# Early weight slabs loaded one step ahead of their split, with their steps spread over both products of a feed-forward half

## The chip, the cores and the metric

The kernel runs on one core of a Trainium2 chip. Its engines are TensorE (PE: matmuls, and PEld: their weight loads), VectorE (DVE), ScalarE (ACT), GpSimd (POOL) and SyncE (SP), each with its own instruction queue, and 16 DMA engines that move data between HBM and the core's memory. The metric is the time of one execution on the device in microseconds, the median of several runs.

## The reference

A decoder trunk of two layers over 256 tokens of width 1024, all in float32. Each layer is a half-step feed-forward block, a mixer of three attention branches, and a second half-step feed-forward block:

```python
def swiglu_ffn(x, g, wi, wo):
    a, b = jnp.split(rms_norm(x, g) @ wi, 2, axis=-1)
    return (jax.nn.silu(a) * b) @ wo

for l in range(DEPTH):
    x = x + 0.5 * swiglu_ffn(x, ffn1_norm[l], ffn1_wi[l], ffn1_wo[l])
    h = rms_norm(x, mix_norm[l])
    ...  # stick-breaking, latent and sparse attention on h @ w_in, gated sum y
    x = x + y @ w_out[l]
    x = x + 0.5 * swiglu_ffn(x, ffn2_norm[l], ffn2_wi[l], ffn2_wo[l])
```

The inner width DFF is 2816, so wi is 1024 x 5632 and wo is 2816 x 1024.

## The kernel before

Precision. Every float32 operand of a matmul is split into a high part, rounded to TensorE's fast float32 type by a copy on ScalarE, and a low part, the rest, by a subtraction on VectorE. A product is then three matmuls (high by high, high by low, low by high) that add up in one PSUM bank. So all weights go through ScalarE and VectorE too, not only through TensorE.

Weights. They stream in a fixed order as slabs of 128 partitions x up to 1024 columns. A slab is loaded in two raw halves of 512 columns (`load_raw`, six buffers named raw) from SyncE's queue, and each half is split into the slab's tiles: whi/wlo from the pool wp, four buffers that live through the whole kernel, or vhi/vlo from the pool fp, four buffers that live for one feed-forward half. `slab_tiles` decides: the slabs 4 to 43 of a half use vhi/vlo, the first four and the 22 slabs of wo use whi/wlo. `next_slab` keeps two slabs loaded beyond the one it gives out. A raw half's buffer is free again when its subtraction on VectorE is done, and a slab's tiles are free when TensorE has used the slab.

A feed-forward half (`ffn`, run four times: two per layer). In words, it has three parts.

- Eight steps: the first 256 columns of both parts of wi (slabs 0 to 3), for each of the two row tiles t of 128 tokens: 24 matmuls of 512 columns each. Behind the last step of a tile, `glu` makes the SiLU on ScalarE (tile sil) and the gate product g on VectorE.
- The first product: five chunks of 512 columns of wi, first the gate part and then the value part of each, so ten drains of four slabs. It runs transposed (`chunk_T`): the weights are stationary, the 256 tokens are the moving operand, and each drain yields eight times (i = 0 to 7) after 12 matmuls of 256 columns. Between two yields a hook may put other work in. For the first drain it puts in `flush` at i = 3 and i = 5 (four transposes in all, that bring g into the transposed layout, split into gh and gl) and `spread_rn` at i = 4: the row scales of the norm are broadcast to a tile rnb on VectorE and transposed, for each row tile in turn; rnb has one buffer, so the second copy waits for the first transpose and the second transpose for the second copy. The result `rows` is what `gate_T` multiplies by at the end of each gate drain.
- The second product (`out_rows`): 22 slabs of wo, 12 matmuls of 512 columns each, with gh and gl stationary.

Early slabs. The mixer's weights are heavy on ScalarE and VectorE, so for ten of its slabs per list in `EARLY_AT` the split is done ahead, in a feed-forward half before it (`split_early`): load a half to eraw, copy to ehi on ScalarE, subtract to elo on VectorE, and store both to HBM from GpSimd's queue. The mixer later loads them straight to whi/wlo. One early half is one step of the generator `ahead`; there are 20 steps in each of the first three feed-forward halves, none in the last. The load is held in SyncE's queue behind the last raw load emitted before it (`issue_after(last_dma[0])`). Before, `hook2` makes a step at i = 2 and i = 6 of every drain (in the very first half not in the first chunk), and `between` makes the four that are left in the first half's second product.

Order. TensorE's order is the program's (`manual_schedule`). In the feed-forward halves a list scheduler with its own estimate of times sets the order on VectorE, ScalarE, GpSimd and SyncE; in the mixer, `Planner` does for VectorE and ScalarE too. The scheduler may move an instruction forward past others of the program.

## Time and profile before

| | |
|---|---|
| median of 3 runs | 1289.9 us (1288.9 to 1293.35) |
| the profiled execution, its time | 1291.65 us |
| its span | 1289.9 us |
| TensorE busy | 1269.0 us (98%) |
| VectorE, ScalarE, GpSimd busy | 917.5, 787.8, 107.4 us |
| matmuls | 8103 records |
| read from HBM, written to it | 257.22 MB, 34.60 MB |

The span runs from the first to the last instruction; the execution's own time has 1.75 us more around it. Busy time of TensorE is counted from the start of a matmul to its modelled end, and neighbours overlap, so a busy TensorE can still start its matmuls at different distances. A row of the time line has the start in us from the span's start, the length, the engine, the line of the kernel, the tiles as out<-in, and in brackets the idle time before it with what ended it. A row of waits has the waiting instruction, what it waited for, the total in us, how often, and the longest.

### The profile page before, as it was taken

How to read it: one execution, taken by the hardware profiler on the slowest of the kernel's cores; microseconds unless marked ns; L12 is line 12 of the kernel's file. 1: busy time of each engine (PE TensorE's matmuls, PEld its weight loads, DVE VectorE, ACT ScalarE, POOL GpSimd, SP SyncE). 2: the span in 40 equal slices, each digit the busy share in tenths (PEclk: the TensorE clock that was granted, in tenths of full speed). 3: DMA queues.
4: the chain of work that ended last, by engine and by line, in shares of the span. 5: the costliest groups of instructions: out<-in, count | busy, mean ns of one | idle time of the engine just before them, and what ended most of it. 6: DMA issues, size and time to landing. Idle time of an engine off the chain costs nothing. (4 is left out here: it accounts for less than half of the span.)

```text
span 1289.9 us, 23603 instructions
## 1 busy us (share of the span) xinstructions
PE 1269.0 (98%) x8103; PEld 1127.0 (87%) x8103; DVE 917.5 (71%) x1934; ACT 787.8 (61%) x1644; POOL 107.4 (8%) x170
## 2 busy tenths in 40 slices
PE   7999999999999999999999999999999999999998
PEld 6999888888877889998889998888888778899987
DVE  6667667888898776776568765679768887666643
ACT  6555557777877565655456664578757774544542
POOL 0112100210000011220012210011100000000000
PEclk9999999999999999999999999999999999999999
DMA  7899876656645568997579996575786455566653
GB/s 234 286 318 324 292 265 219 196 168 218 205 126 170 168 230 299 338 328 247 177 263 345 326 323 198 187 228 157 246 289 223 141 168 166 180 183 193 214 164 115
DMA packets 151401, 293.93 MB, mean 228 GB/s; under 512 B 17768, under 2 KB 19440, under 8 KB 151280
## 3 DMA queue, kind: packets, MB, share of 16 engines
q1 hardware_dynamic: 141424, 260.43, 62.8%
q0 software_dynamic: 9856, 31.99, 6.6%
q8 instruction: 63, 1.03, 0.3%
q14 instruction: 58, 0.48, 0.1%
HBM read 257.22 MB, written 34.60 MB: 226 GB/s over the span
## 5 line engine op out<-in xcount | busy, mean ns | idle before, releaser
L758 PE MATMUL acc<-hThi,vhi 128*128 128x256 f32 x1280 | 356.7, 279 | 0.0
L760 PE MATMUL acc<-hThi,vlo 128*128 128x256 f32 x1280 | 356.5, 279 | 0.0
L759 PE MATMUL acc<-hTlo,vhi 128*128 128x256 f32 x1280 | 355.9, 278 | 0.0
L539 DVE TENSOR_TENSOR vlo<-raw,vhi 128x512 fp32r<-128x512 f32 x320 | 207.5, 686 | 62.5 <-ACT vhi L538 59.9
L538 ACT ACTIVATE vhi<-raw 128x512 fp32r<-128x512 f32 x320 | 188.4, 623 | 91.7 <-PE acc L759 35.5
L759 PEld LDWEIGHTS acc<-hTlo,vhi 128*128 128x128 f32 x1280 | 240.5, 188 | 0.1
L758 PEld LDWEIGHTS acc<-hThi,vhi 128*128 128x128 f32 x1280 | 240.3, 188 | 0.2
L760 PEld LDWEIGHTS acc<-hThi,vlo 128*128 128x128 f32 x1280 | 240.1, 188 | 0.3 <-DVE vlo L539 0.2
L539 DVE TENSOR_TENSOR wlo<-raw,whi 128x512 fp32r<-128x512 f32 x240 | 155.1, 686 | 110.4 <-ACT whi L538 110.0
L538 ACT ACTIVATE whi<-raw 128x512 fp32r<-128x512 f32 x240 | 138.7, 622 | 125.2 <-PE acc L586 94.7
L584 PE MATMUL acc<-whi,hThi 128*128 128x512 f32 (+2 forms) x480 | 189.9, 396 | 0.0
L586 PE MATMUL acc<-whi,hTlo 128*128 128x512 f32 (+2 forms) x480 | 184.6, 385 | 0.1
L585 PE MATMUL acc<-wlo,hThi 128*128 128x512 f32 (+2 forms) x480 | 183.9, 383 | 0.2 <-DVE wlo L539 0.2
L979 DVE TENSOR_TENSOR wlo<-raw,whi 128x512 fp32r<-128x512 f32 x216 | 141.0, 679 | 25.6 <-ACT whi L977 24.5
L977 ACT ACTIVATE whi<-raw 128x512 fp32r<-128x512 f32 x216 | 126.3, 617 | 39.0 <-PE acc L586 22.5
L584 PE MATMUL acc<-whi,gh 128*128 128x512 f32 x352 | 137.6, 391 | 0.0
L586 PE MATMUL acc<-whi,gl 128*128 128x512 f32 x352 | 137.0, 389 | 0.0
L585 PE MATMUL acc<-wlo,gh 128*128 128x512 f32 x352 | 137.0, 389 | 0.0
L586 PEld LDWEIGHTS acc<-whi,hTlo 128*128 128x128 f32 x480 | 90.6, 189 | 18.9 <-DVE ss L590 0.9
L584 PEld LDWEIGHTS acc<-whi,hThi 128*128 128x128 f32 x480 | 91.0, 190 | 15.7 <-issue 1.1
L585 PEld LDWEIGHTS acc<-wlo,hThi 128*128 128x128 f32 x480 | 91.1, 190 | 14.5 <-DVE wlo L539 0.6
L565 ACT ACTIVATE ehi<-eraw 128x512 fp32r<-128x512 f32 x60 | 37.8, 630 | 103.1 <-DMA eraw<-in_wts 102.8
(305 smaller groups left out, 1872.3 us busy)
## 6 DMA issues: line engine op xcount, KB each, us to landing
raw<-in_wts SPq DMA_DIRECT2D x764, 256.0 KB, 3.1
eraw<-in_wts SPq DMA_DIRECT2D x60, 256.0 KB, 5.3
early<-ehi POOLq DMA_DIRECT2D x60, 256.0 KB, 4.2
early<-elo POOLq DMA_DIRECT2D x60, 256.0 KB, 4.8
whi<-early SPq DMA_DIRECT2D x60, 256.0 KB, 4.0
wlo<-early SPq DMA_DIRECT2D x60, 256.0 KB, 3.9
gain<-in_gains SPq DMA_DIRECT2D x5, 512.0 KB, 5.7
xd<-x SPq DMA_DIRECT2D x4, 512.0 KB, 4.3
```

The source lines that it names most:

```text
L538: nc.scalar.activation(hi[:, c:c + m], raw[:, :m], AF.Copy)
L539: nc.vector.tensor_tensor(lo[:, c:c + m], raw[:, :m], hi[:, c:c + m], op=OP.subtract)
L565: nc.scalar.activation(hi, raw, AF.Copy)
L584: nc.tensor.matmul(o, a[0], b[0], start=start, stop=False)
L585: nc.tensor.matmul(o, a[0], b[1], start=False, stop=False)
L586: nc.tensor.matmul(o, a[1], b[0], start=False, stop=stop)
L758: nc.tensor.matmul(o, sl[0][:, w], h, start=k == 0 and c == 0, stop=False)
L759: nc.tensor.matmul(o, sl[0][:, w], l_, start=False, stop=False)
L760: nc.tensor.matmul(o, sl[1][:, w], h, start=False, stop=k == KT - 1 and c == 1)
L977: nc.scalar.activation(hl[0][:, c:c + m], raw[:, :m], AF.Copy)
L979: nc.vector.tensor_tensor(hl[1][:, c:c + m], raw[:, :m], hl[0][:, c:c + m], op=OP.subtract)
```

## The change

Five edits, all for the feed-forward halves.

1. `split_early` is one step deeper: a step loads its half and then finishes (copy, subtraction, stores) the half that the step before loaded. One more step at the end finishes the last, so there are 21.
2. The steps are placed anew: one per drain (i = 6) in the first three chunks, two per drain (i = 2 and 6) in the last two, and one at every odd slab k < 18 of the second product.
3. `spread_rn` comes first at i = 3 of the first drain, and both flushes directly after it.
4. Slab 6 of a half uses whi/wlo instead of vhi/vlo.
5. The first vhi, the tile rows and the first vlo are allocated at the start of the half, and slab 4 takes them.

```diff
@@ -501,7 +501,7 @@
 
     last_dma = [None]
     fpool = [None]
-    rows = [None]
+    own = []
 
     def slab_at(i):
         l, j = stream[i]
@@ -511,13 +511,11 @@
 
 
         j = stream[i][1] % (len(plan) - FFN_SLABS)
-        if not 4 <= j < FFN_SLABS - DFF // 128:
+        if not 4 <= j < FFN_SLABS - DFF // 128 or j == 6:
             return tuple(wp.tile([128, 1024], R, tag=t, name=t) for t in ("whi", "wlo"))
-        fp = fpool[0]
-        hi = fp.tile([128, 1024], R, tag="vhi", name="vhi", bufs=W_BUFS)
-        if rows[0] is None:
-            rows[0] = fp.tile([128, 320], F, name="rows", bufs=1)[:, 0:S].rearrange("p (t n) -> p t n", t=NT)
-        return hi, fp.tile([128, 1024], R, tag="vlo", name="vlo", bufs=W_BUFS)
+        if own:
+            return own.pop()
+        return tuple(fpool[0].tile([128, 1024], R, tag=t, name=t, bufs=W_BUFS) for t in ("vhi", "vlo"))
 
     def load_raw(base, c, m):
         raw = wp.tile([128, RAW], F, tag="raw", name="raw", bufs=RAW_BUFS)
@@ -551,23 +549,30 @@
 
     def split_early(fp, l, part):
 
+        def finish(i, c, raw):
+            d = dp.tile([2, 128, 512], F, tag=f"early{i}_{c}", name="early")
+            hi, lo = fp.tile([128, 512], R, tag="ehi", name="ehi"), fp.tile([128, 512], R, tag="elo", name="elo")
+            nc.scalar.activation(hi, raw, AF.Copy)
+            nc.vector.tensor_tensor(lo, raw, hi, op=OP.subtract)
+            nc.gpsimd.dma_start(d[0], hi.bitcast(F))
+            nc.gpsimd.dma_start(d[1], lo.bitcast(F))
+            early.setdefault(i, []).append(d)
+
+        held = None
         for a in EARLY_AT[part]:
             i = l * len(plan) + FFN_SLABS + a
             base, n, _ = slab_at(i)
             assert n == 1024
-            early[i] = []
             for c in range(0, n, 512):
                 raw = fp.tile([128, 512], F, tag="eraw", name="eraw")
                 with tc.issue_after(last_dma[0]):
                     nc.sync.dma_start(raw, wts[base + 128 * c:base + 128 * (c + 512)].rearrange("(p n) -> p n", p=128))
-                d = dp.tile([2, 128, 512], F, tag=f"early{i}_{c}", name="early")
-                hi, lo = fp.tile([128, 512], R, tag="ehi", name="ehi"), fp.tile([128, 512], R, tag="elo", name="elo")
-                nc.scalar.activation(hi, raw, AF.Copy)
-                nc.vector.tensor_tensor(lo, raw, hi, op=OP.subtract)
-                nc.gpsimd.dma_start(d[0], hi.bitcast(F))
-                nc.gpsimd.dma_start(d[1], lo.bitcast(F))
-                early[i].append(d)
+                if held:
+                    finish(*held)
+                held = i, c, raw
                 yield
+        finish(*held)
+        yield
 
     def next_slab():
         while pos[0] < len(stream) and len(ready) < 1 + AHEAD:
@@ -706,11 +711,13 @@
         hT = of_t(hq)
         with ExitStack() as es:
             fp = fpool[0] = es.enter_context(tc.tile_pool(name="fp", bufs=2))
-            rows[0] = None
             gq = (fp.tile([128, 96 + DFF * NT], R, name="gh", bufs=1)[:, 96:].rearrange(
                       "p (k t n) -> p k t n", t=NT, n=128),
                   fp.tile([128, DFF * NT + 48], R, name="gl", bufs=1)[:, :DFF * NT].rearrange(
                       "p (k t n) -> p k t n", t=NT, n=128))
+            vhi = fp.tile([128, 1024], R, tag="vhi", name="vhi", bufs=W_BUFS)
+            rows = fp.tile([128, 320], F, name="rows", bufs=1)[:, 0:S].rearrange("p (t n) -> p t n", t=NT)
+            own.append((vhi, fp.tile([128, 1024], R, tag="vlo", name="vlo", bufs=W_BUFS)))
             gT = [(gq[0][:, :, t, :], gq[1][:, :, t, :]) for t in range(NT)]
             todo = []
             ahead = split_early(fp, l, 0) if gi == 0 else split_early(fp, l + 1, 1) if l + 1 < depth else iter(())
...
@@ -855,14 +862,15 @@
                     step(i)
 
             def hook(i):
-                if i in (3, 5):
-                    flush()
-                if i == 4 and ci == 0:
-                    spread_rn()
+                if i == 3:
+                    if ci == 0:
+                        spread_rn()
+                    while todo:
+                        flush()
                 hook2(i)
 
             def hook2(i):
-                if i in (2, 6) and (l or gi or ci):
+                if i == 6 and (l or gi or ci) or i == 2 and ci >= 3:
                     next(ahead, None)
 
             for ci, (f0, fn) in enumerate(FFN_CHUNKS[1:]):
@@ -879,7 +887,7 @@
                 drain(chunk_T(fn, value_T), hook2)
 
             def between(k):
-                if k in (5, 7, 9, 11):
+                if k % 2 and k < 18:
                     next(ahead, None)
             out_rows(gT, DFF // 128, between, last=l == depth - 1 and gi == 2, by=rn)
 
```

What this does to the queues, first at the start of the second feed-forward half (the first layer's second one) on ScalarE, before: sil is the SiLU of `glu`, once per row tile; ehi is the copy of an early half; gh is the copy of a transposed gate.

```order
427 L720 ACT_TABLE_LOAD
428 L720 ACTIVATE sil<-acc,rn 128x256
429 L538 ACTIVATE vhi<-raw 128x512
430 L565 ACTIVATE ehi<-eraw 128x512
431 L720 ACTIVATE sil<-acc,rn 128x256
432 L565 ACTIVATE ehi<-eraw 128x512
433 L538 ACTIVATE vhi<-raw 128x512 x4
434 L579 ACTIVATE gh<-tp 128x2x128
435 L565 ACTIVATE ehi<-eraw 128x512
436 L743 ACTIVATE rows<-tp 128x256
```

And after:

```order
421 L727 ACT_TABLE_LOAD
422 L727 ACTIVATE sil<-acc,rn 128x256
423 L536 ACTIVATE vhi<-raw 128x512 x2
424 L536 ACTIVATE whi<-raw 128x512 x2
425 L536 ACTIVATE vhi<-raw 128x512
426 L555 ACTIVATE ehi<-eraw 128x512
427 L727 ACTIVATE sil<-acc,rn 128x256
428 L536 ACTIVATE vhi<-raw 128x512 x4
429 L750 ACTIVATE rows<-tp 128x256
430 L584 ACTIVATE gh<-tp 128x2x128 x2
431 L555 ACTIVATE ehi<-eraw 128x512
```

Between the two SiLUs there are now two more vhi copies and the two whi copies of slab 6 ahead of the early copy; the early copy that stood behind the second SiLU is gone, as is the one ahead of rows, and both gate copies stand together.

VectorE at the same place, before: vlo and wlo are the low parts of raw halves, elo of an early half, gl of a gate, rn the row scales.

```order
613 L539 TENSOR_TENSOR vlo<-raw,vhi 128x512 x2
614 L722 TENSOR_TENSOR g<-acc,sil 128x256
615 L633 TENSOR_SCALAR rn<-rs 128x1 x3
616 L539 TENSOR_TENSOR vlo<-raw,vhi 128x512
617 L566 TENSOR_TENSOR elo<-eraw,ehi 128x512
618 L722 TENSOR_TENSOR g<-acc,sil 128x256
619 L566 TENSOR_TENSOR elo<-eraw,ehi 128x512
620 L539 TENSOR_TENSOR vlo<-raw,vhi 128x512 x4
621 L580 TENSOR_TENSOR gl<-tp,gh 128x2x128
622 L741 COPY rnb<-rn 128x128
623 L566 TENSOR_TENSOR elo<-eraw,ehi 128x512
624 L539 TENSOR_TENSOR vlo<-raw,vhi 128x512 x2
```

And after:

```order
613 L729 TENSOR_TENSOR g<-acc,sil 128x256
614 L537 TENSOR_TENSOR vlo<-raw,vhi 128x512
615 L638 TENSOR_SCALAR rn<-rs 128x1 x3
616 L537 TENSOR_TENSOR vlo<-raw,vhi 128x512
617 L537 TENSOR_TENSOR wlo<-raw,whi 128x512 x2
618 L537 TENSOR_TENSOR vlo<-raw,vhi 128x512
619 L556 TENSOR_TENSOR elo<-eraw,ehi 128x512
620 L729 TENSOR_TENSOR g<-acc,sil 128x256
621 L537 TENSOR_TENSOR vlo<-raw,vhi 128x512 x2
622 L748 COPY rnb<-rn 128x128
623 L537 TENSOR_TENSOR vlo<-raw,vhi 128x512 x2
624 L585 TENSOR_TENSOR gl<-tp,gh 128x2x128 x2
```

The split gl stood ahead of the copy rnb (this is the second copy, the first stands further up); now two splits vlo stand ahead of rnb, and both gl behind it.

SyncE from the start of the same half, before: raw are the raw halves, eraw the early ones.

```order
118 L524 DMA raw<-in_wts 128x512 x36
119 L562 DMA eraw<-in_wts 128x512
120 L524 DMA raw<-in_wts 128x512 x4
121 L562 DMA eraw<-in_wts 128x512
122 L524 DMA raw<-in_wts 128x512 x4
123 L562 DMA eraw<-in_wts 128x512
124 L524 DMA raw<-in_wts 128x512 x4
125 L562 DMA eraw<-in_wts 128x512
```

And after:

```order
118 L522 DMA raw<-in_wts 128x512 x40
119 L569 DMA eraw<-in_wts 128x512
120 L522 DMA raw<-in_wts 128x512 x8
121 L569 DMA eraw<-in_wts 128x512
122 L456 DMA gain<-in_gains 128x1024
123 L522 DMA raw<-in_wts 128x512 x8
124 L569 DMA eraw<-in_wts 128x512
```

The first early load stands four raw loads later, and eight raw loads lie between two early ones instead of four. From the middle of the first product on the distance is four again, now into the second product.

## Rows read from the trace of the kernel before

**Rows 1.** The page: busy us of each engine, share, instructions.

```profile
PE 1269.0 (98%) x8103; PEld 1127.0 (87%) x8103; DVE 917.5 (71%) x1934; ACT 787.8 (61%) x1644; POOL 107.4 (8%) x170
```

**Rows 2.** Waits of TensorE: who waits for whom, us, times, longest.

```profile
PE tp L742 <- DVE rnb L741: 2.8, 4, 0.7
```

**Rows 3.** Time line, TensorE, start and length in us, where products begin.

```profile
23.33 0.28 PE L758 MATMUL acc<-hThi,vhi 128*128 128x256 f32 x1
...
135.82 0.40 PE L584 MATMUL acc<-whi,gh 128*128 128x512 f32 x1
...
474.26 0.28 PE L758 MATMUL acc<-hThi,vhi 128*128 128x256 f32 x1
...
584.93 0.40 PE L584 MATMUL acc<-whi,gh 128*128 128x512 f32 x1
...
1110.94 0.28 PE L758 MATMUL acc<-hThi,vhi 128*128 128x256 f32 x1
...
1225.60 0.40 PE L584 MATMUL acc<-whi,gh 128*128 128x512 f32 x1
```

**Rows 4.** Windows: length, PE, PEld, DVE, ACT, POOL busy (x), clock, DMA, GB/s.

```profile
40.00:60.00 20.00, 20.00 (x179) 20.00 (x178) 14.78 (x42) 9.43 (x17) 2.36 (x4) 1.00 0.89 294
102.00:122.00 20.00, 20.00 (x172) 19.99 (x171) 13.21 (x22) 10.89 (x21) 3.78 (x7) 1.00 0.98 335
500.00:520.00 20.00, 20.00 (x179) 20.00 (x179) 15.57 (x26) 13.19 (x24) 4.32 (x8) 1.00 0.93 325
1150.00:1170.00 20.00, 20.00 (x172) 20.00 (x171) 12.79 (x21) 9.66 (x18) 0.00 (x0) 1.00 0.63 186
```

**Rows 5.** Time line, TensorE, in the first half's first product.

```profile
99.38 0.28 PE L759 MATMUL acc<-hTlo,vhi 128*128 128x256 f32 x1
99.62 0.39 PE L760 MATMUL acc<-hThi,vlo 128*128 128x256 f32 x1
```

**Rows 6.** Waits, whole span, of ScalarE and of SyncE's queue.

```profile
ACT ehi L565 <- DMA eraw<-in_wts: 102.8, 44, 4.6
...
SPq L524 <- DVE vlo L539: 268.3, 276, 6.0
```

**Rows 7.** Time line, second half: TensorE at the rnb pair, VectorE beside it.

```profile
481.56 0.27 PE L742 MATMUL tp<-ident,rnb 128*128 128x128 f32 x1
482.53 0.33 PE L742 MATMUL tp<-ident,rnb 128*128 128x128 f32 x1 [0.70 <-DVE rnb L741]
...
481.92 0.42 DVE L580 TENSOR_TENSOR gl<-tp,gh 128x256 fp32r<-128x256 f32 x1
482.26 0.22 DVE L741 COPY rnb<-rn 128x128 f32<-128x128 f32 x1
```

**Rows 8.** DMA issues (64:129, then 463:482 us): count, KB, median to landing.

```profile
eraw<-in_wts SPq DMA_DIRECT2D x12, 256.0 KB, 5.9
...
eraw<-in_wts SPq DMA_DIRECT2D x3, 256.0 KB, 4.1
```

**Rows 9.** Time line, start of the second half: SyncE, TensorE, then ScalarE.

```profile
467.72 0.33 SPq L562 DMA_DIRECT2D eraw<-in_wts  x1
...
470.16 0.39 PE L584 MATMUL acc<-whi,hThi 128*128 128x512 f32 x1
...
471.30 0.48 ACT L720 ACTIVATE sil<-acc,rn 128x256 f32<-128x256 f32 x1
471.67 0.62 ACT L538 ACTIVATE vhi<-raw 128x512 fp32r<-128x512 f32 x1
472.19 0.62 ACT L565 ACTIVATE ehi<-eraw 128x512 fp32r<-128x512 f32 x1
474.46 0.48 ACT L720 ACTIVATE sil<-acc,rn 128x256 f32<-128x256 f32 x1 [1.65 <-PE acc L586]
```

**Rows 10.** Windows in the second product, first half and second half.

```profile
140.00:190.00 50.00, 50.00 (x222) 41.41 (x221) 29.75 (x48) 25.13 (x45) 4.32 (x8) 1.00 0.82 274
588.00:638.00 50.00, 50.00 (x223) 41.39 (x221) 27.03 (x43) 23.26 (x41) 0.00 (x0) 1.00 0.69 220
```

More of the change, by code (lines that the diff above doesn't have):

```diff
@@ L742, in spread_rn @@
                     nc.tensor.transpose(tp[:, t * 128:(t + 1) * 128], b, ident)
-                nc.scalar.activation(rows[0].rearrange("p t n -> p (t n)"), tp[:, 0:S], AF.Copy)
+                nc.scalar.activation(rows.rearrange("p t n -> p (t n)"), tp[:, 0:S], AF.Copy)
             def chunk_T(n, evac):
@@ L767, in gate_T @@
                 nc.vector.tensor_tensor(s.rearrange("p (c n) -> p c n", c=2), a.rearrange("p (c n) -> p c n", c=2),
-                                        rows[0].rearrange("p t n -> p (t n)")[:, None, :].to_broadcast([128, 2, S]),
+                                        rows.rearrange("p t n -> p (t n)")[:, None, :].to_broadcast([128, 2, S]),
                                         op=OP.mult)
```

## The prediction

> **What bounds the kernel now.** I read the page's busy shares first, then the list of waits, then the time line of TensorE in the stage that the change touches, and the other engines only where TensorE stands beside them. TensorE is busy for 1269.0 of 1289.9 us [rows 1]: it sets the time, and a change elsewhere counts only if it alters a wait of TensorE or the pace at which its matmuls start. Its waits are few. In the feed-forward stages there are four for the second spread of the row scales (rnb, one in each first product, 2.8 us together) [rows 2]. ScalarE's 102.8 us of waits for the raw halves of early slabs [rows 6] cost TensorE nearly nothing, because a slab's split is made some slabs ahead of its use.
>
> The second thing to see is the pace. All four first products run the same 960 matmuls of 256 columns, yet from their first matmul to the first one of the second product it takes 135.82-23.33 = 112.49 us, 584.93-474.26 = 110.67 us and 1225.60-1110.94 = 114.66 us [rows 3]. In 20 us of such a product there are 179 matmuls in one stretch and 172 in another, both at clock 1.00 [rows 4]: the engine has two paces at one clock, about 112 and 116 ns from start to start by these counts. A short wait changes the pace. At 99.62 us a matmul comes 0.24 us after the one before [rows 5]; the first product is fast between 40 and 60 us and slow between 102 and 122 [rows 4]. The first product of the second half, past its rnb wait at 482.53 us [rows 7], is fast between 500 and 520 us, the last slow between 1150 and 1170 [rows 4]. The whole of a first product in the fast pace is worth 114.66-110.67 = 4.0 us. In this execution two of the four took it after the rnb wait (the first one lost it again at 99.6 us), two did not. The third, not shown, is like the last.
>
> **The change part by part.** The profiled execution took 1291.65 us in all for a span of 1289.9, so 1.75 us lie around the span; the median of the three timed runs is 1289.9, which is 1.75 less. I work out terms against the profiled execution and carry their sum to the median.
>
> *Matmuls, splits, loads, stores.* Their counts are the same: 60 early halves, each with one load, one ScalarE copy, one VectorE subtraction and two stores. What moves is when. The second product of a feed-forward half now carries nine steps in three of the halves, where before only the first had four. 50 us of the second product hold 222 matmuls with such steps (140 to 190 us) and 223 without them (588 to 638 us) [rows 10]; one record in 222 tells no difference. So I cost the move at 0: the cover is that VectorE and ScalarE are busy for only 29.75 and 25.13 of those 50 us. If that cover were gone, each half split late would cost TensorE its 0.6 us on VectorE.
>
> *The load one step ahead.* It is emitted one step earlier, but the scheduler then places the copy of a half (ehi) on ScalarE by its own estimate of the landing. Counted along the queues, before: the copy comes after the splits of all raw halves but two of those loaded ahead of its early load in 48 of 60 cases and of all but four in 7; after: in 37, of all but four in 15 and of all but six in 2. A raw load waits until VectorE has done the split six halves earlier (SyncE's largest wait, 268.3 us in 276 times, [rows 6]), so an early load issued later against an unchanged queue gives ScalarE less lead, not more. I expect ScalarE's waits for early halves to stay between 75 and 130 us. On TensorE this is worth 0 where three slabs of lead remain.
>
> *The copy in front of the second SiLU.* At the start of the second and third feed-forward halves it does touch TensorE's path. Before, the early half was loaded at 467.72 us and copied at 472.19 us, free of any wait, and the SiLU of the second row tile ran at 474.46 us, when its product was ready [rows 9]. After, the load stands four raw halves later on SyncE, and the last of them needs the buffer of the seventh slab, which is now split into whi/wlo. That buffer comes free with the fifth step, at 470.16 us [rows 9]. From the first SiLU at 471.30 us, four splits of 0.52 us (the spacing 471.67 to 472.19, [rows 9]) bring the seventh slab's copies to 473.8 us, VectorE to about 474.5, the raw load and the early load to 475.5 (0.5 us each, an estimate from the 0.33 us that an early load stands on SyncE at 467.72, [rows 9]). A load that lands in 4.1 us, the median there [rows 8], arrives at 479.6. Only then come the copy, the SiLU (480.1), two splits on ScalarE (to 481.6) and on VectorE (to 482.3), and behind them the second rnb copy; TensorE starts the second transpose at 482.6. It reaches the first one at the fourth hook, 474.26 + 48 x 0.119 (114.66/960) = 480.0. The gap is then 2.6 us, against 482.53-481.56 = 0.97 now [rows 7], so +1.6. In the order of after one split fewer stands ahead of the first SiLU, and the third half loads no table there; if all of it comes by two splits (1.0 us) earlier it is +0.6. I take +1.0 in each of two halves, +2.0. Bounds for each: -0.33 if the SiLU is not held up (next term), +3.4 if the load takes 5.9 us, the median in the crowded stretch of the first half [rows 8].
>
> *The rnb pair first.* In the order before, the split of the transposed gates (gl) stands ahead of the second rnb copy on VectorE. The first transpose ends at 481.83; the copy starts at 482.26, after gl from 481.92 [rows 7]. After, gl stands behind it. With VectorE idle the copy would start about 0.1 us after the transpose, 0.33 earlier. That applies where no early copy stands ahead of it: the first and the last half, -0.66 in all. If a split (0.6 us) is in the way instead, it is +0.27 each. In the first half the second gate g follows the rnb copy on VectorE; its 0.42 us lie beside two transposes of TensorE. The merged transposes cost the same per piece.
>
> *The wait at 99.6 us* ends in the same order in both kernels, with a lighter load just before; half a chance of losing its 0.24 us: -0.1. The seventh slab in the other pool needs no wait of TensorE: its split is done before the first product begins, 2 slabs ahead of use. The order in both mixers is unchanged on every engine.
>
> Sum: +2.0-0.66-0.1 = +1.2. Against the profiled execution 1292.9, carried to the median 1291.1; I say 1291.
>
> The Trainium skill, "DMA: Bandwidth & Descriptors", section "Latency and other measured facts", says that an access to HBM takes 0.2 us on average and up to 2 us under high load, and that a lighter load makes a transfer's fixed part smaller. The trace agrees in sign: 5.9 against 4.1 us at landing. By the rule, with the early traffic thinned to one step in eight halves, the wait before the SiLU would shrink by up to 1.8 us and its term would fall to about -0.3 in each half, a total of -1.4 and 1288.5, about the time of the last rival below.
>
> **The rivals.**
> *The fast pace is taken more often.* Every rnb wait starts the pace anew, and after it there now stand four transposes more. For it: after a wait both paces occurred here. Against it: transposes without a wait left the pace as it was, in both kinds. If the last two halves take it, 2 x 4.0 us, and the first keeps it to its end (135.82-99.84 = 36 us, 7 of 179 matmuls, 1.4 us), the time is 1291-9.4 = 1281.6; with one half more than now, 1287; the middle is 1284.5.
> *The fast pace is not taken at all* (the slower side, one mechanism). For it: the wait at 99.6 us ended in the slow pace [rows 5], and so did the rnb wait of two halves. The place is the matmul after the four g transposes; the price is 4.0 us in the second half and about 66 us x 7/179 = 2.6 us in the first, so 1291 + 6.6 = 1297.6. It decides from the point at which fewer than one half in four is fast: with one instead of two lost, 1295.
> *ScalarE stands longer at the early copy.* If the loads land in 5.9 us, the two starts cost up to 3.4 us each instead of 1.0: 1291 + 4.8 = 1295.8, and 1294.5 from the middle. For it: the same load took 5.9 us where the traffic was dense. Against it: the 4.1 us measured at that very place [rows 8].
> *The change does not load ahead in effect,* and the placing of the SiLU turns out as before: -0.33 four times and nothing else, 1288.6. For it: the scheduler moves the copies freely; against it: the order already shows the copy in front.
>
> **How the numbers follow.** The forecast has 0.46 (1289 to 1293.5), no effect of loading ahead 0.14, the fast pace more often 0.16, no fast pace 0.12, longer waits at the early copy 0.12. 0.3% of 1289.9 is 3.9 us, about what a measurement of this kernel can tell from no change: faster is below 1286.0, slower above 1293.8. Faster: most of the fast-pace case and a little of the forecast, 0.17. Slower: the two slow cases but for their lower ends, and the forecast's upper end, 0.24. The rest, 0.59, is no change. The range reaches from the middle of the fast-pace case to the middle of the slow ones, 1285.5 to 1296.0.
>
> **What would show it.** In the trace of after, the rnb wait of TensorE in the second and third first products is about 2 us from transpose to transpose and the SiLU before it is released by the early half's copy; in the first and the last it is about 0.65 us. ScalarE's waits for early halves remain near 100 us. The second products hold 222 or 223 matmuls in 50 us with the steps, as before. Wrong would be: SiLU at its old place in both, waits of TensorE for splits of more than 1 us in the first products, or a mixer that differs by more than 2 us. Whether one or two halves run at the fast pace is read from the 20 us counts, 179 or 172.

## The result, and the profile after

The changed kernel takes 1279.43 us, the median of 6 runs (1278.84 to 1280.43), against 1289.4 for the kernel before (6 runs, 1284.67 to 1293.35) on the same chip: a ratio of 0.9929, 95% interval 0.9908 to 0.995. That is faster, by about 10 us; the forecast was 1291.0, its range 1285.5 to 1296.0. The profiled execution took 1280.09 us for a span of 1278.3. The page's line of busy times, answering to [rows 1]:

```profile
PE 1259.6 (99%) x8103; PEld 1117.9 (87%) x8103; DVE 918.4 (72%) x1934; ACT 785.3 (61%) x1644; POOL 108.0 (8%) x170
```

TensorE's busy time fell by 9.4 us, and the span by 11.6. The first matmuls of the products say where (time line, answering to [rows 3]):

```profile
23.33 0.28 PE L765 MATMUL acc<-hThi,vhi 128*128 128x256 f32 x1
...
134.04 0.40 PE L589 MATMUL acc<-whi,gh 128*128 128x512 f32 x1
...
472.54 0.28 PE L765 MATMUL acc<-hThi,vhi 128*128 128x256 f32 x1
...
582.90 0.40 PE L589 MATMUL acc<-whi,gh 128*128 128x512 f32 x1
...
1104.16 0.28 PE L765 MATMUL acc<-hThi,vhi 128*128 128x256 f32 x1
...
1214.53 0.40 PE L589 MATMUL acc<-whi,gh 128*128 128x512 f32 x1
```

In the order of the halves, the first products take 110.71, 110.36, 110.36 (the third, not shown) and 110.37 us here; they took 112.49, 110.67, 114.65 and 114.66. That is 10.7 of the 11.6 us. The rest of the kernel differs by at most 0.5 us in any one part. The windows that stood in [rows 4], of the changed kernel:

```profile
40.00:60.00 20.00, 20.00 (x179) 20.00 (x178) 16.64 (x44) 11.09 (x21) 1.28 (x2) 1.00 0.71 219
102.00:122.00 20.00, 20.00 (x179) 20.00 (x178) 13.79 (x24) 12.05 (x22) 3.79 (x7) 1.00 0.92 323
500.00:520.00 20.00, 20.00 (x178) 20.00 (x178) 14.08 (x23) 12.01 (x22) 2.17 (x4) 1.00 0.78 257
1150.00:1170.00 20.00, 20.00 (x179) 20.00 (x179) 12.50 (x21) 10.64 (x19) 0.00 (x0) 1.00 0.67 199
```

Now 178 or 179 matmuls stand in each of the four stretches, at clock 1.00, the two that held 172 included. So the first, second and fourth halves are in the fast pace, and the third, whose product takes as long, is too. The next view shows where it begins: TensorE in the second half, at the end of the seventh slab (whi, wlo) and the start of the eighth (vhi, vlo).

```profile
481.90 0.28 PE L765 MATMUL acc<-hThi,whi 128*128 128x256 f32 x1
482.02 0.28 PE L766 MATMUL acc<-hTlo,whi 128*128 128x256 f32 x1
482.14 0.28 PE L767 MATMUL acc<-hThi,wlo 128*128 128x256 f32 x1
482.26 0.28 PE L765 MATMUL acc<-hThi,vhi 128*128 128x256 f32 x1
482.38 0.28 PE L766 MATMUL acc<-hTlo,vhi 128*128 128x256 f32 x1
482.49 0.28 PE L767 MATMUL acc<-hThi,vlo 128*128 128x256 f32 x1
482.61 0.28 PE L765 MATMUL acc<-hThi,vhi 128*128 128x256 f32 x1
```

In the seventh slab the matmuls start 0.12 us apart; from the second matmul of the eighth slab on 0.11 or 0.12, as the two decimals of this view round it. From here on a pace is the mean distance from start to start over the 24 matmuls of a slab, worked out from the same time line and leaving out the distance behind a transpose. In all four halves of the changed kernel it is 117.8 ns in the fifth and sixth slab, about 120 in the seventh, slower than either pace that the prediction knew, and 113.3 in each of the 37 slabs behind it, from the second matmul of the eighth slab on. In the kernel before, the slabs of these products ran at 117.8 or 113.3 where no matmul came late. (The prediction's 116 and 112 ns came from counts, and a count of a stretch takes in the matmuls that lie across its edges.)

The waits of TensorE for the row scales, answering to [rows 2], and the place itself in the second half, answering to [rows 7]:

```profile
PE tp L749 <- DVE rnb L748: 1.3, 4, 0.3
```

```profile
478.20 0.27 PE L749 MATMUL tp<-ident,rnb 128*128 128x128 f32 x1
478.79 0.33 PE L749 MATMUL tp<-ident,rnb 128*128 128x128 f32 x1 [0.32 <-DVE rnb L748]
...
478.51 0.23 DVE L748 COPY rnb<-rn 128x128 f32<-128x128 f32 x1 [0.52 <-PE tp L749]
```

From transpose to transpose it takes 0.59 us (0.97 before); the four halves give 0.62, 0.59, 0.59 and 0.59, together 1.5 us less; the other 9.2 of the 10.7 us are pace. What stood ahead of it, on SyncE and ScalarE, with the landing of the early loads from 463 to 482 us (count, KB, median us), answering to [rows 9] and [rows 8]:

```profile
472.21 0.33 SPq L569 DMA_DIRECT2D eraw<-in_wts  x1
...
469.91 0.47 ACT L727 ACTIVATE sil<-acc,rn 128x256 f32<-128x256 f32 x1
470.28 1.14 ACT L536 ACTIVATE vhi<-raw 128x512 fp32r<-128x512 f32 x2
471.33 1.14 ACT L536 ACTIVATE whi<-raw 128x512 fp32r<-128x512 f32 x2
472.37 0.62 ACT L536 ACTIVATE vhi<-raw 128x512 fp32r<-128x512 f32 x1
475.10 0.63 ACT L555 ACTIVATE ehi<-eraw 128x512 fp32r<-128x512 f32 x1 [2.10 <-DMA eraw<-in_wts]
475.63 0.46 ACT L727 ACTIVATE sil<-acc,rn 128x256 f32<-128x256 f32 x1
```

```profile
eraw<-in_wts SPq DMA_DIRECT2D x2, 256.0 KB, 2.9
```

The early load was issued at 472.21 us and its copy began at 475.10, and the second SiLU stood behind that copy, as the order said. But it began at 475.63, 2.6 us ahead of the first row scale's transpose at 478.20. ScalarE's waits for early loads over the span, with SyncE's largest, answering to [rows 6], and the second products, answering to [rows 10]:

```profile
ACT ehi L555 <- DMA eraw<-in_wts: 115.5, 53, 5.8
SPq L522 <- DVE vlo L537: 255.4, 268, 6.6
```

```profile
140.00:190.00 50.00, 50.00 (x222) 41.42 (x221) 32.07 (x51) 27.47 (x49) 8.13 (x15) 1.00 0.92 328
588.00:638.00 50.00, 50.00 (x222) 41.40 (x221) 28.42 (x45) 24.56 (x44) 5.42 (x10) 1.00 0.82 282
```

### The profile page after: what moved, and what is told of

The parts are those of the page before. It is cut to its first block, busy times and chain, and to the rows that moved or that the text cites. A ratio compares the mean times of both kernels' runs of the same rounds, so it can differ in the third digit from the quotient of the medians.

```text
span 1278.3 us, 23581 instructions
## 1 busy us (share of the span) xinstructions
PE 1259.6 (99%) x8103; PEld 1117.9 (87%) x8103; DVE 918.4 (72%) x1934; ACT 785.3 (61%) x1644; POOL 108.0 (8%) x170
## 4 chain that ended last, share of the span: by engine, by line
PE 89%; DVE 4%; ACT 3%; issue 2%; DMA 1%; POOL 0%; SPq 0%; DVEq 0%; ACTq 0%
PE acc L589 16%; PE acc L591 16%; PE acc L590 16%; PE acc L767 11%; PE acc L766 11%; PE acc L765 11%; PE tp L1551 1%; DVE x L675 1%; ACT wf L1510 1%; DVE vlo L537 1%; PE att L1903 1%; PE att L1460 1%; PE tp L1579 1%; DVE wlo L537 1%; DMA zc<-wf 1%
## 5 line engine op out<-in xcount | busy, mean ns | idle before, releaser
L767 PE MATMUL acc<-hThi,vlo 128*128 128x256 f32 x1248 | 344.7, 276 | 0.0
L766 PE MATMUL acc<-hTlo,vhi 128*128 128x256 f32 x1248 | 344.7, 276 | 0.0
L765 PE MATMUL acc<-hThi,vhi 128*128 128x256 f32 x1248 | 344.6, 276 | 0.0
L536 ACT ACTIVATE vhi<-raw 128x512 fp32r<-128x512 f32 x312 | 182.0, 621 | 98.9 <-PE acc L766 38.6
L537 DVE TENSOR_TENSOR vlo<-raw,vhi 128x512 fp32r<-128x512 f32 x312 | 202.4, 685 | 51.6 <-ACT vhi L536 50.5
L766 PEld LDWEIGHTS acc<-hTlo,vhi 128*128 128x128 f32 x1248 | 234.3, 188 | 0.2
L765 PEld LDWEIGHTS acc<-hThi,vhi 128*128 128x128 f32 x1248 | 234.3, 188 | 0.2
L767 PEld LDWEIGHTS acc<-hThi,vlo 128*128 128x128 f32 x1248 | 234.3, 188 | 0.0
L537 DVE TENSOR_TENSOR wlo<-raw,whi 128x512 fp32r<-128x512 f32 x248 | 159.9, 684 | 83.9 <-ACT whi L536 83.5
L987 DVE TENSOR_TENSOR wlo<-raw,whi 128x512 fp32r<-128x512 f32 x216 | 140.9, 678 | 25.4 <-ACT whi L985 24.2
L555 ACT ACTIVATE ehi<-eraw 128x512 fp32r<-128x512 f32 x60 | 37.9, 631 | 116.7 <-DMA eraw<-in_wts 115.5
L556 DVE TENSOR_TENSOR elo<-eraw,ehi 128x512 fp32r<-128x512 f32 x60 | 41.5, 691 | 93.1 <-ACT ehi L555 92.9
L589 PEld LDWEIGHTS acc<-whi,hThi 128*128 128x128 f32 x480 | 91.0, 190 | 15.6 <-issue 1.1
```

What stands on the lines that cost most here:

```text
L536: nc.scalar.activation(hi[:, c:c + m], raw[:, :m], AF.Copy)
L537: nc.vector.tensor_tensor(lo[:, c:c + m], raw[:, :m], hi[:, c:c + m], op=OP.subtract)
L555: nc.scalar.activation(hi, raw, AF.Copy)
L556: nc.vector.tensor_tensor(lo, raw, hi, op=OP.subtract)
L589: nc.tensor.matmul(o, a[0], b[0], start=start, stop=False)
L765: nc.tensor.matmul(o, sl[0][:, w], h, start=k == 0 and c == 0, stop=False)
```

## The experiments

Theory A at the outset: the seventh slab, split into other buffers, sets the pace of all slabs behind it. Rival B: the hook order does (row scales first, then four transposes together). Rival C: the spread of the early steps does. The table gives, for each kernel, the median and range of its runs, the ratio to the kernel before on the same chip with its 95% interval, and the lengths of the four first products in its profile (from the first matmul of one product to that of the next, as in [rows 3]). The runs are from several series, beside which the kernel before took 1287.19 to 1293.59 us in the median (both on the chip of runs 13 to 18). So a ratio depends on the paces that the kernel before had in that series, and kernels of different series are compared by their first products. Such a product lasts 110.4 us with the fast pace from the eighth slab on, 114.3 without it.

| run | us | ratio | first products, us |
|---|---|---|---|
| changed kernel | 1279.43 (1278.84 to 1280.43) | 0.9929 (0.9908 to 0.995) | 110.7, 110.4, 110.4, 110.4 |
| 1 without the seventh slab | 1294.65 (1290.96 to 1298.53) | 1.0023 (1.001 to 1.0035) | 114.3, 114.3, 114.3, 114.3 |
| 2 seventh slab alone | 1306.0 (1305.25 to 1307.95) | 1.0119 (1.0097 to 1.0141) | 114.7, 118.8, 119.6, 114.7 |
| 3 hook order alone | 1294.69 (1291.55 to 1297.05) | 1.0025 (1.0012 to 1.0037) | 114.3, 114.3, 114.3, 114.3 |
| 4 slab 24 instead | 1287.37 (1286.55 to 1289.66) | 0.997 (0.9954 to 0.9985) | 112.3, 112.3, 112.3, 112.3 |
| 5 seventh slab and hook order | 1284.6 (1281.49 to 1289.68) | 0.9939 (0.9917 to 0.9962) | 110.6, 114.9, 115.9, 110.4 |
| 6 transposes between | 1295.78 (1294.2 to 1297.3) | 1.0017 (1.0003 to 1.0032) | 114.5, 114.3, 114.3, 114.3 |
| 7 addresses alike | 1304.42 (1303.12 to 1306.04) | 1.0092 (1.0067 to 1.0117) | 116.4, 116.4, 116.4, 116.4 |
| 8 early steps alone | 1295.75 (1289.5 to 1299.19) | 1.0025 (1.0006 to 1.0043) | 114.6, 114.7, 111.9, 114.7 |
| 9 to 12, offsets 32, 64, 128, 192 | 1297.48, 1278.84, 1298.15, 1295.21 (one run each) | | 114.8; 110.0 and 110.2; 115.2; 114.3 |
| 13 offset 64, timed | 1278.43 (1278.13 to 1285.0) | 0.994 (0.9917 to 0.9962) | 110.6, 114.3, 110.2, 110.2 |
| 14 changed kernel, series of 13 | 1279.62 (1278.39 to 1280.58) | 0.9938 (0.9918 to 0.9957) | 110.4, 110.4, 110.4, 110.4 |
| 15 before with offset 64 | 1292.89 (1287.24 to 1297.58) | 1.0038 (1.0021 to 1.0054) | 112.8, 110.7, 114.7, 110.7 |
| 16 vhi 64, vlo 192 | 1278.95 (one run) | | 110.0, 110.0, 110.9, 110.0 |
| 17 the same, timed | 1279.21 (1278.65 to 1280.9) | 0.988 (0.986 to 0.99) | 111.7, 110.0, 111.2, 110.0 |
| 18 and the seventh slab | 1279.57 (1278.23 to 1281.0) | 0.9885 (0.9866 to 0.9904) | 110.7, 110.2, 110.2, 110.2 |

**Run 1**, edit 4 undone.

```diff
-        if not 4 <= j < FFN_SLABS - DFF // 128 or j == 6:
+        if not 4 <= j < FFN_SLABS - DFF // 128:
```

> The changed kernel, but the seventh slab of a feed-forward half is split into vhi/vlo again (only edit 4 undone). Theory A: the seventh slab's other buffers put every following slab into the fast pace (113.3 ns from start to start), in all four halves. Then without it each half is slow (117.8 ns) or fast as the rnb wait leaves it: a slow half costs 37 slabs x 24 matmuls x 4.5 ns = 4.0 us, so 1279.4 plus 0 to 16 us, and with one or two fast halves, as before, 1287 to 1292, with halves in both paces or a change of pace within one. Rival B: the row scales first and the four gate transposes right behind them set the fast pace: 1279.4 within 1 us, all four halves fast. Rival C: the spread of the early steps does it: 1279.4 within 1 us too.

```profile
500.00:520.00 20.00, 20.00 (x173) 20.00 (x172) 12.88 (x22) 10.41 (x19) 2.17 (x4) 1.00 0.77 252
```

All four halves ran at 117.8 to their ends (173 matmuls in the window above, where the changed kernel has 178), and the kernel is no faster than before, but 0.2% slower. B and C fall as causes by themselves: without the seventh slab the rest of the change gains nothing.

**Run 2**, edit 4 alone in the kernel before.

```diff
-        if not 4 <= j < FFN_SLABS - DFF // 128:
+        if not 4 <= j < FFN_SLABS - DFF // 128 or j == 6:
```

> The kernel before with edit 4 alone: the seventh slab in whi/wlo. Theory A: all four halves fast from the eighth slab on, about 120 ns in the seventh; the time is that of the changed kernel plus the 1.4 us that the shorter rnb waits brought there: 1280.8, 1280 to 1282. Rivals B and C: 1289 within 2 us, two or three halves still slow.

Theory A in this form was wrong too, by 25 us. The seventh slab ran at 120 and the slabs behind it at 117.8. Besides, TensorE stood for the second row scale (time line, ScalarE, TensorE and VectorE, second half):

```profile
478.34 0.63 ACT L565 ACTIVATE ehi<-eraw 128x512 fp32r<-128x512 f32 x1 [1.95 <-DMA eraw<-in_wts]
483.25 0.63 ACT L565 ACTIVATE ehi<-eraw 128x512 fp32r<-128x512 f32 x1 [3.23 <-DMA eraw<-in_wts]
...
482.80 0.27 PE L742 MATMUL tp<-ident,rnb 128*128 128x128 f32 x1
486.33 0.33 PE L742 MATMUL tp<-ident,rnb 128*128 128x128 f32 x1 [3.26 <-DVE rnb L741]
...
486.05 0.22 DVE L741 COPY rnb<-rn 128x128 f32<-128x128 f32 x1
```

The early copies (ehi) stand in ScalarE's queue ahead of what the row scales need, and wait 1.95 and 3.23 us for their loads. Behind the second one follow its elo, two splits and gl on VectorE, and only then the copy rnb at 486.05; so TensorE waits 3.26 us. The window behind it (columns as in [rows 4]):

```profile
486.00:491.00 5.00, 4.67 (x27) 4.68 (x28) 0.69 (x3) 0.77 (x3) 0.00 (x0) 0.66 0.87 309
```

The granted clock is 0.66 here, a mixture of the two levels 1.2 and 2.4 GHz, after TensorE had stood; the matmuls there start 0.21 us apart instead of 0.12. In the third half the wait was 4.1 us. What was still missing for the pace: in the order of before, two gate transposes stand exactly between the seventh slab and the eighth.

**Run 3**, edit 3 alone in the kernel before.

```diff
-                if i in (3, 5):
-                    flush()
-                if i == 4 and ci == 0:
-                    spread_rn()
+                if i == 3:
+                    if ci == 0:
+                        spread_rn()
+                    while todo:
+                        flush()
```

> The kernel before with edit 3 alone: the row scales at the third hook, both flushes right behind. Theory A: 0.35 us less at each rnb wait, 1.4 us in all, and the pace as it falls: 1284 to 1292, halves in both paces. Rival B: all four halves fast behind these transposes, 1279.5 within 1.5 us. Rival C: 1288 with the halves as before.

1294.69: slow in all four halves, and above the 1284 to 1292 that A gave. The rnb waits did shrink as in the changed kernel (1.3 us together), but the mixture of paces that the kernel before has behind them was gone, in favour of the slow one.

**Run 4**, the changed kernel with another slab in whi/wlo.

```diff
-        if not 4 <= j < FFN_SLABS - DFF // 128 or j == 6:
+        if not 4 <= j < FFN_SLABS - DFF // 128 or j == 24:
```

> The changed kernel with slab 24 of a half (counted from 0) in whi/wlo instead of slab 6. Theory A: slabs 6 to 23 slow or fast as it falls, slab 24 at about 120 ns, slabs 25 to 43 at 113.3 in all four halves; a half that starts slow costs 18 x 24 x 4.5 ns = 1.9 us, so 1279.4 to 1287.2. Rivals B and C: fast from slab 7 on in all halves, or no change of pace behind slab 24.

```profile
500.00:520.00 20.00, 20.00 (x172) 20.00 (x171) 12.97 (x21) 10.53 (x19) 2.16 (x4) 1.00 0.76 257
560.00:580.00 20.00, 20.00 (x179) 20.00 (x178) 14.02 (x23) 11.12 (x21) 3.70 (x7) 1.00 0.95 338
```

172 matmuls ahead of slab 24, 179 behind it, in the second half; in each of the four halves 117.8 until slab 23, 119.6 in slab 24, 113.3 from slab 25 on. 1287.37 is the upper end that A gave, 1287.2. So the slab in whi/wlo is the switch, at both places where it was tried.

**Run 5**, edits 3 and 4 in the kernel before (the diffs of runs 2 and 3 together).

> The kernel before with edits 3 and 4 (hook order and seventh slab), the early steps as before. Theory A, narrowed: the fast pace comes in where a slab of vhi/vlo follows a slab of whi/wlo with no other matmul in between, which edit 4 alone lacked (two gate transposes stood there). Then slabs 7 to 43 run at 113.3 ns in all four halves. The early copies still wait for their loads ahead of the row scales in the second and third halves, so TensorE stands about 3 us in each, as with the seventh slab alone, and the clock falls for a while behind it: some 4 us each, 1279.4 + 8 = 1287, 1284 to 1290. Rival C (the spread of the early steps is needed for the pace): slabs 7 to 43 at 117.8, 1303.

113.3 right behind the seventh slab in all four halves, so edit 3 is what edit 4 needed. The time lies in the expected range, but not for the reason given: the 3 us for the row scales did not come (rnb waits 1.3 us together). What came instead, in the second and third halves, begins on ScalarE (time line, ScalarE, VectorE, TensorE):

```profile
498.29 0.63 ACT L565 ACTIVATE ehi<-eraw 128x512 fp32r<-128x512 f32 x1 [6.04 <-DMA eraw<-in_wts]
...
498.95 0.69 DVE L566 TENSOR_TENSOR elo<-eraw,ehi 128x512 fp32r<-128x512 f32 x1 [5.73 <-ACT ehi L565]
500.76 0.68 DVE L539 TENSOR_TENSOR vlo<-raw,vhi 128x512 fp32r<-128x512 f32 x1
...
501.10 0.28 PE L759 MATMUL acc<-hTlo,vhi 128*128 128x256 f32 x1
501.50 0.39 PE L760 MATMUL acc<-hThi,vlo 128*128 128x256 f32 x1
501.73 0.28 PE L758 MATMUL acc<-hThi,vhi 128*128 128x256 f32 x1
```

The early copy waits 6.04 us for its load and VectorE's elo for the copy; so the split vlo at 500.76 us ends late, and the matmul that needs it starts 0.40 us after the one before. The windows ahead of this wait and behind it:

```profile
485.00:499.00 14.00, 14.00 (x126) 14.00 (x125) 4.96 (x9) 5.58 (x11) 1.08 (x2) 1.00 0.75 265
517.00:531.00 14.00, 14.00 (x122) 14.00 (x121) 11.57 (x20) 9.55 (x18) 3.25 (x6) 1.00 0.97 319
```

At the same clock there are 126 matmuls in 14 us ahead and 122 behind: 113.3 ns had become 117.8. In the third half waits of this kind (the two halves have seven in TensorE's list of waits, 3.1 us) turned the pace from fast to slow and back several times. In the changed kernel no first product waits for a split; so edits 1 and 2 protect the pace (edit 5 is the only other difference). In this profile, which is of the slowest of the six runs (1289.68), that is worth 10 us; the medians, from two series, differ by 5. Which of the two edits does it was not tried.

**Run 6**, the changed kernel with two transposes between the seventh slab and the eighth again.

```diff
                 if i == 3:
                     if ci == 0:
                         spread_rn()
-                    while todo:
-                        flush()
+                    flush()
+                if i == 5:
+                    flush()
```

> The changed kernel, but two of the four gate transposes stand at the fifth hook again, that is between the seventh slab (whi/wlo) and the eighth (vhi/vlo); all else as in the changed kernel. Theory A, narrowed: the direct passage from one slab to the other is gone, slabs 7 to 43 at 117.8 in all four halves or as it falls: 1291 to 1295. Rival (the seventh slab's own slower matmuls set the pace whatever stands behind them): 113.3 in all four, 1279.4 within 1 us.

```profile
500.00:520.00 20.00, 20.00 (x172) 20.00 (x172) 13.27 (x21) 11.24 (x21) 2.17 (x4) 1.00 0.71 242
```

172 matmuls, 117.8 in all four halves, 1295.78. The seventh slab's own 120 ns does not bring the fast pace; the passage from whi/wlo straight into vhi/vlo does.

**Run 7**, the changed kernel with the same instructions at other addresses.

```diff
-                  fp.tile([128, DFF * NT + 48], R, name="gl", bufs=1)
+                  fp.tile([128, DFF * NT], R, name="gl", bufs=1)
...
-            rows = fp.tile([128, 320], F, name="rows", bufs=1)
+            rows = fp.tile([128, 256], F, name="rows", bufs=1)
```

> The changed kernel with the same instructions in the same order, but two pads in front of vhi and vlo left out (48 columns behind gl, and 64 of the tile rows), so that all vhi and vlo lie at multiples of 1024 bytes in a partition, as whi and wlo do. Theory A1: the 120 ns of the seventh slab come from where its tiles lie. Then all slabs run at 120 and no change of pace is left: 4 halves x (37 x 24 x 6.7 ns + 2 x 24 x 2.2 ns) = 24 us more, 1303. Rival A2: they come from the change of buffers itself, whatever the addresses: seventh slab at 120, then 113.3, 1279.4 within 1 us.

```profile
500.00:520.00 20.00, 20.00 (x169) 20.00 (x168) 13.79 (x23) 11.03 (x21) 2.16 (x4) 1.00 0.75 241
```

169 matmuls: 119.7 to 120.0 in every slab of all four halves, and 1304.42 where 1303 was expected. The pace of the seventh slab is a matter of where its tiles lie: whi and wlo lie at multiples of 1024 bytes, vhi and vlo 192 and 448 bytes past one, in the kernel before as in the changed one. The pads move the other tiles that lie behind them too (rows, gates, early halves).

**Run 8**, edits 1 and 2 alone in the kernel before: `split_early` as in the change, and

```diff
-                if i in (2, 6) and (l or gi or ci):
+                if i == 6 and (l or gi or ci) or i == 2 and ci >= 3:
...
-                if k in (5, 7, 9, 11):
+                if k % 2 and k < 18:
```

> The kernel before with edits 1 and 2 alone (the load one step ahead, the steps spread over both products). Theory A: no pace of its own; each half fast or slow as the rnb wait leaves it, 1286 to 1296, rnb waits of 0.6 to 1.0 us from transpose to transpose. Rival C (the spread sets the pace): all four halves fast, 1280.

Three halves slow, one fast behind its rnb wait, 1295.75 with runs from 1289.5 to 1299.19, as theory A had it; rnb waits of 2.8 us, as before. So the two edits that the title names gain nothing by themselves.

**Runs 9 to 12**, the changed kernel without edit 4 and with other pads, one run each. The first of them, the others in the same way:

```diff
-                  fp.tile([128, DFF * NT + 48], R, name="gl", bufs=1)
+                  fp.tile([128, DFF * NT + 8], R, name="gl", bufs=1)
...
-            rows = fp.tile([128, 320], F, name="rows", bufs=1)
+            rows = fp.tile([128, 256], F, name="rows", bufs=1)
```

> The changed kernel without edit 4 and with other pads: vhi and vlo lie 32 bytes past a multiple of 1024 (8 columns behind gl, tile rows 256 columns wide). Theory A1 (the tiles' addresses set which paces there are): one pace from slab 4 on that may be neither 113.3 nor 117.8 nor 120.0 ns, the same in all four halves. Rival (every offset but 0 has the two paces): 117.8 in all four, as without the seventh slab, 1294.6.

> As the run with 32 bytes, at 64 bytes past a multiple of 1024. Theory A1: one pace in all four halves, another than at 32 if the distance counts in steps of 64. Rival: 117.8 in all four.

> As the run with 32 bytes, at 128 bytes past a multiple of 1024. Theory A1: a pace between 113 and 120 in all four halves; if it is 113.3 from slab 4 on, 1294.6 - 4 x 40 x 24 x 4.5 ns = 1277.3. Rival: 117.8 in all four.

> The changed kernel without edit 4, vhi and vlo both 192 bytes past a multiple of 1024 (vhi as in the changed kernel, vlo moved from 448 to 192 by the narrower tile rows). Theory A1: if a distance of 256 bytes makes no difference, 117.8 in all four halves and 1294.6, as without the seventh slab alone; if it does, another pace. Rival: 117.8.

Behind the rnb wait, at 32 bytes 118.3 ns, at 128 between 118.5 and 118.8, at 192 117.8, each in all four halves, and at 64 113.3 in all four, with no seventh slab at all. At 32, 64 and 128 the paces differ, as A1 had it; the 117.8 at 192 was expected from both sides.

**Runs 13 to 16.** The 64 byte kernel timed, the changed kernel on the same chip, the kernel before with nothing but these pads, and vhi and vlo at different distances (the last; its pads are below).

```diff
-                  fp.tile([128, DFF * NT + 48], R, name="gl", bufs=1)
+                  fp.tile([128, DFF * NT + 16], R, name="gl", bufs=1)
...
-            rows = fp.tile([128, 320], F, name="rows", bufs=1)
+            rows = fp.tile([128, 288], F, name="rows", bufs=1)
```

> The kernel of the run with 64 bytes again, now timed beside the changed kernel: no seventh slab in whi/wlo, vhi and vlo 64 bytes past a multiple of 1024. If the address alone gives the fast pace behind every rnb wait: about 0.1 us per half below the changed kernel, whose seventh slab runs at 120 and not at 113.3 (24 x 6.7 ns = 0.16 us): 0.6 us below it, and no run above 1282. If the first look was one of two outcomes: single runs of 1283 to 1295 among them.

> The changed kernel itself on the chip of the other runs of this call, so that they can be compared with it: 1279.4 within 1.5 us, every run in the fast pace behind the seventh slab.

> The kernel before with nothing but the two pads changed, so that vhi and vlo lie 64 bytes past a multiple of 1024; the same instructions in the same order. If the address decides what a wait leaves behind: 113.3 ns behind the rnb wait in all four halves, 1278.8 + 1.4 for the longer rnb waits = 1280.2 (1279 to 1283, the upper end for short waits in mid-product). Rival (the hook order, row scales first, is needed as well): halves in both paces, 1284 to 1294.

> As the run with 64 bytes, but vlo at 192 bytes past a multiple of 1024 and vhi at 64. If the place of the high parts decides (two of three weight loads): 113.3 in all four halves behind the rnb wait. If that of the low parts does: 117.8. If the two must stand alike: a third pace.

Five of the six runs of the 64 byte kernel lie between 1278.13 and 1278.73; the sixth, the profiled one, took 1285.0, with the second half at 117.8 throughout, which is 4 of its 6.6 us. So this address favours the fast pace without fixing it. In the kernel before the pads alone bring nothing: 1292.89 where 1280.2 was expected, three halves fast and one slow even in the profile of its fastest run (1287.24). With vhi at 64 and vlo at 192 the fifth and sixth slabs too ran at 113.3 to 114.2, in all four halves.

Runs 12 and 16 differ in nothing but the place of vhi and of rows, 192 bytes against 64, with vlo at 192 in both (windows of run 12, then of run 16):

```profile
500.00:520.00 20.00, 20.00 (x172) 20.00 (x171) 12.83 (x22) 11.26 (x21) 2.16 (x4) 1.00 0.77 257
500.00:520.00 20.00, 20.00 (x178) 20.00 (x178) 14.30 (x23) 11.10 (x21) 1.64 (x4) 1.00 0.84 280
```

In all four halves 117.8 ns became 113.3. TensorE does not read rows in these products, so the place of the high parts is enough to change the pace, in one run of each, on two chips.

**Runs 17 and 18.** That last kernel timed, and with the seventh slab in whi/wlo besides.

> The kernel of the run with vhi at 64 and vlo at 192 bytes, now timed: edits 1, 2, 3 and 5 and the new pads, no seventh slab in whi/wlo. If this place is fast from slab 4 on whatever stood before, every run is within 1 us of its median, and the median is below the changed kernel's by 3 slabs x 24 x 4.5 to 6.7 ns = 0.4 us in each half: 1278. If the one look was luck: single runs 4 us higher for each half that takes the slow pace.

> The changed kernel, seventh slab in whi/wlo included, with the pads of the run beside it. If the passage from whi/wlo to vhi/vlo gives the fast pace at these addresses too: 113.3 ns in slabs 7 to 43 of all halves and a spread of runs within 1 us, 24 x 6.7 ns = 0.16 us in each half above the run beside it: 0.6 us above it. If it does not: 117.8 behind slab 6, up to 4 us more for each half.

Every half of both is at 113.3 ns behind the place of the seventh slab, and the runs agree within 3 us. In the profile of run 17 two splits came late (waits, TensorE):

```profile
PE acc L767 <- DVE vlo L537: 1.8, 2, 0.9
```

With such a wait the pace stayed at 113.3 here. Both medians are within 0.5 us of the changed kernel's two (1279.43 and 1279.62), so no version was found that is clearly faster than it. The 1278 expected of run 17 did not come.

## Why the prediction was wrong

**The step that failed** is this one: "The seventh slab in the other pool needs no wait of TensorE: its split is done before the first product begins, 2 slabs ahead of use." It costed edit 4 by waits alone, at 0. There is indeed no wait, but not for the reason given. In the second half the seventh slab's last split (VectorE) ran past the start of the first product at 472.54 us:

```profile
472.33 1.28 DVE L537 TENSOR_TENSOR wlo<-raw,whi 128x512 fp32r<-128x512 f32 x2
```

It ended at 473.6 us, 5.7 us before TensorE used the slab at 479.31. (The prediction's own times, VectorE at 474.5 against a first product at 474.26, also put the split's end behind the start.) What the edit does is on TensorE itself: other addresses, another pace in that slab, and, with edit 3, the fast pace behind it. Run 1 against the changed kernel prices it by the first products: 3.9 us in each half (114.3 - 110.4), 15.6 in all. The spans of the two profiles differ by 14.2 us, the medians, from two series, by 15.2.

**The pace taken for chance.** The two paces and their price (4.0 us for a first product) were read rightly, but "Every rnb wait starts the pace anew" was made a matter of luck. In the kernel before it looks like that: its halves differ, and its runs spread over 9 us. But the orders with the row scales first had a definite outcome at these addresses: slow in all halves without the passage from one pool to the other (runs 1, 3 and 6), fast behind it (the changed kernel, runs 4 and 14, and run 5 until a split came late). With the old hook order it stayed mixed (run 8). The rival with the fast pace taken more often had the right sign; it asked that the last two halves take the fast pace and the first keep it, at a chance of 0.16, and this came. But it put it down to the rnb wait and the four transposes behind it, which in runs 1 and 3 led to the slow pace. Its 1281.6 is the nearest of the numbers given; as to the cause, that is luck. The rival without the fast pace named the four transposes behind the rnb wait, and for edit 3 alone it was right: run 3, four slow halves.

**The copy in front of the second SiLU** was put at +2.0 for two halves. The order was read rightly, the times were not: the early load was issued at 472.21 us (473.9 by the clock of the kernel before, whose second half begins 1.7 us later), not at 475.5, and it landed in 2.9 us, not 4.1. It did not wait for the seventh slab's split, as the prediction had it: it was issued before that split began (472.33). The bound without a hold-up held. The Trainium skill's rule that the prediction set against this term ("DMA: Bandwidth & Descriptors", "Latency and other measured facts": a lighter load makes a transfer's fixed part smaller) has the 2.9 on its side, and its -1.4 is close to the -1.5 that the waits gave; no run here separates the load from the earlier issue. That an early copy can hold up the row scales is shown by run 2, where one behind the second SiLU did, with the load not one step ahead: 3.26 us in the second half and 4.1 in the third.

**The rnb pair first** was put at -0.66 in two halves; it came in all four, at -0.31 to -0.39 each, -1.5 together: the right size, in two halves more.

**The wait at 99.6 us** was put at -0.1. No matmul comes late there in the changed kernel, and the fast pace lasts past it: of the 1.8 us that the first half's first product gained, 0.3 are its rnb wait and 1.5 the pace kept to the end.

**Loading one step ahead** was put at 0, and ScalarE's waits between 75 and 130 us; they are 115.5. Run 8 shows no gain from it alone. But beside edits 3 and 4 the 0 was wrong: without edits 1 and 2 (run 5) late splits end the fast pace in two halves, at 4.6 and 5.6 us with the waits themselves (114.92 and 115.94 against 110.36). The prediction named a split's 0.6 us as the price of a lost cover, and not the pace that goes with it.

**What held:** the second products with 222 matmuls in 50 us, the mixers within 0.5 us, the start of a half. Of what the first products gained, the shorter rnb waits are 1.5 us; the rest came from a place without any wait.

## What to carry to other kernels

Where matmuls of one form run at several start distances at one granted clock, ask what distinguishes the stretches before calling it chance: the operands' addresses, and what ran directly ahead. An edit that only moves a weight tile to another buffer is costed on TensorE's pace too, and 4.5 ns are 16 us where there are 3552 matmuls (37 slabs x 24 x 4). A set of edits is tested in its parts and in pairs: here edit 4 alone was 1.2% slower, edit 3 alone 0.25% slower, the two together 0.6% faster, and the whole change 0.7%. Edit 5 was not tried alone.

## What the runs showed of the hardware

- The same matmuls of 256 columns, each with its own weight load, start 113.3, 117.8, 118.3, about 118.7 or 120.0 ns apart at clock 1.00, by the place of the weights in a partition: with vhi and vlo at multiples of 1024 bytes 119.7 to 120.0 in every slab of run 7; at 32 and 128 bytes past one, 118.3 and about 118.7 in one run each; with vhi at 64 and the changed order, mostly 113.3 (runs 10, 13, 16 to 18).
- At some places two paces last: at 192 and 448 bytes 113.3 and 117.8. Behind the rnb wait of the kernel before either came, and no row shows why; the passage below and late matmuls set it. It then held for up to 37 slabs (888 matmuls). A matmul that came late (0.24 to 1.0 us behind the one before) could change it, in both directions, as in run 5, and did not always.
- A passage straight from weights at 0 bytes (120 ns) to weights at 192 and 448 set the fast one in every half seen, 16 halves of the profiles of the changed kernel (twice) and of runs 4 and 5; two transposes in between undid it in all four halves of run 6.
- Why the places differ, and what of the weight load and the moving operand meets where, no row shows; that it is a conflict of the two reads is only a guess. The other tiles that the pads move are ruled out as a cause only between runs 12 and 16, where all but vhi and rows lie alike. Nor is it shown why the kernel before, with the weights at 64 bytes, still had a slow half.
